# The expert layer's down product in plain f32 with stationary weights, with four weight and six activation buffers

## The chip, the core and the metric

The kernel runs on one NeuronCore of one Trainium2 chip. The metric is device time in microseconds of one launch, as the median of repeated runs. Engine names are those of the profile: PE is TensorE's matmul row and PEld its weight loads, DVE is VectorE, ACT is ScalarE, POOL is GpSimd, SP is the engine that issues most transfers.

## What is computed

Two transformer blocks on 256 tokens of width 2048, in f32: a hybrid mixer, then the expert layer (PEER), then a block with a pooling branch and a block with sparse attention. The change is in the expert layer. Cut to what matters:

```
hn = rms_norm(h) * gain                                  # 256 x 2048
idx, gates = top-k routing of hn @ w_query               # 8 heads x 16 experts of 16384
u = expert_down[idx]                                     # rows of 16384 x 2048
act = gelu(einsum('thkd,td->thk', u, hn))
out = einsum('thk,thkd->td', gates * act, expert_up[idx])
h = h + out
```

## The kernel before

Matmul operands are f32 values, split for speed: `split_w` (lines 149 to 165) loads a weight tile of 128 x 4 x 512 (1 MB) into a buffer `wr`, rounds it with ACT to a high part `wh` in the type float32r, and lets DVE subtract that from the original to get the low part `wl`, in two halves of 128 x 1024 each. Activations exist as a high and a low part too. `mm3` (line 167) then makes three matmuls, low x high, high x low, high x high, with the activations stationary (128 x 128) and 512 weight columns moving.

In the expert layer the first 192 tokens (TD) are computed densely over all 16384 experts, and the other 64 by gathering the rows of their chosen experts (`gathers`: indirect transfers on POOL's queue, a 128 x 2048 row tile each from the pool `fm`, 64 of the down rows, then 64 of the up rows, each consumed by one DVE instruction, lines 780 and 795). The dense part has 32 down chunks (`down`) of 512 experts, each four weight tiles long (2048 rows in four groups of 512), and 16 `up` blocks, each eight weight tiles long. Tokens 0 to 127 take `mm3`. Tokens 128 to 191 are only 64, so their high and low parts stand side by side in one stationary operand of 128 columns (`pack_hn` makes these, in three tiles of `fm`), and two matmuls do for four products (`product2`, lines 199 to 221): 20 matmuls of 512 columns per weight tile. The result has tokens on partitions. ACT copies it out with each token's normaliser (`inv`, and `inv_pair` for the paired layout), and `down_post` transposes it into expert-major form on PE, the pair folded by a matmul against `ff`, before ACT's Gelu writes it. The first seven pairs of chunks (LAG = 7) go out to DRAM (`S`, "hidden") on SP's queue and come back later; the others stay in the pool `gl`.

A gate table for the dense tokens is built by `gate_table` (DVE comparisons, PE products, 12 writes to DRAM) after the routing (`topk`, DVE for the most part). `prep` multiplies it into the activations and splits them for `up`.

Order: after the query product, 18 down chunks (72 tiles), during which routing, gate table and the first gathers run; then seven times an up block followed by two down chunks; then nine up blocks. Instructions are put in order by a planner which takes program order as priority, lets each engine run ahead where its inputs and buffers are ready in its own estimate of time, and issues weight transfers early (`high_priority`). On the chip each engine then keeps that order. A step between weight tiles (`step`, line 223) drives the routing, the gathers (PUMP) and the modulation weights of the second block (`mod_steps`), whose tiles share the `wr` buffers. Buffers before: `wr` 3, `wh` and `wl` 3 halves each, `fm` 7, `gl` 6, and four PSUM accumulators.

Of the kernel before, what the change touches and what calls it, by code (L numbers as in the profile page):

```python
# [10 lines left out]
F32 = mybir.dt.float32  # L11
# [4 lines left out]
AF = mybir.ActivationFunctionType  # L16
OP = mybir.AluOpType
# [4 lines left out]
T = 256  # L22
# [5 lines left out]
TD = 192  # L28
# [9 lines left out]
class Kern:  # L38
    def __init__(self, tc, ctx, d):
        self.tc, self.nc, self.d = tc, tc.nc, d  # L40
        pool = lambda name, bufs, **kw: ctx.enter_context(tc.tile_pool(name=name, bufs=bufs, **kw))
        self.cst = self.ph = pool("cst", 1)
        self.wr = pool("wr", 3)
        self.whp = pool("wh", 3)
        self.wlp = pool("wl", 3)
        self.fmp = pool("fm", 7)
        self.gl = pool("gl", 6)
        self.s4 = pool("s4", 4)
        self.s2 = pool("s2", 4)
        self.sm = pool("sm", 2)  # L50
        self.k1 = pool("k1", 4)
        self.mdp = pool("md", 1)
        self.accp = pool("acc", 4, space=PSUM)
        self.trp = pool("tr", 2, space=PSUM)
        self.msp = pool("ms", 2, space=PSUM)
        self.cnt = 0
        self.consts()
        self.mods = self.mod_steps()
        self.posts, self.seq, self.bg_rate, self.bg_due, self.nmods = [], [], 0.0, 0.0, 0
        self.pump, self.credit = None, 0.0  # L60
# [88 lines left out]
    def split_w(self, wsrc, i):  # L149
        nc = self.nc  # L150
        wr = self.wr.tile([128, 4, 512], F32, tag="wr", name=self.nm("wr"))
        hp = self.tc.high_priority(offset=self.prio)
        hp.__enter__()
        nc.sync.dma_start(wr.rearrange("p k n -> p (k n)"), wsrc[i])
        hs, ls = [], []
        for j in range(2):
            s = slice(2 * j, 2 * j + 2)
            wh = self.whp.tile([128, 2, 512], F32R, tag="wh", name=self.nm("wh"))
            nc.scalar.activation(wh, wr[:, s], AF.Copy)  # L159
            wl = self.wlp.tile([128, 2, 512], F32R, tag="wl", name=self.nm("wl"))  # L160
            nc.vector.tensor_tensor(wl, wr[:, s], wh.bitcast(F32), op=OP.subtract)  # L161
            hs += [wh[:, 0], wh[:, 1]]
            ls += [wl[:, 0], wl[:, 1]]
        hp.__exit__(None, None, None)
        return hs, ls

    def mm3(self, ps, xh, xl, wh, wl, first, last):
        mm = self.nc.tensor.matmul
# [635 lines left out]
    def peer(self, h):  # L804
# [5 lines left out]
        nc.vector.tensor_reduce(s1, self.ss_hn, axis=AX.X, op=OP.add)  # L810
        inv = self.c([128, 2], "inv2")
        self.rinv(inv, s1, 2, 1.0 / D)
        invp = self.c([128, 1], "inv_pair")
        nc.gpsimd.dma_start(invp[0:64], inv[0:64, 1:2])
        nc.gpsimd.dma_start(invp[64:128], inv[0:64, 1:2])
        R = self.c([128, 3, 2, 128], "route")
        ff = self.t_k1([128, 192])
        nc.gpsimd.memset(ff, 0.0)
# [4 lines left out]
        S = self.tc.dram_tile([LAG, 128, 8, TD], F32, name="hidden")  # L823
        C, act = {}, {}

        def down_post(c, tm):
            yield
            i, q = c // 2, c % 2
            if i < LAG:
# [1 line left out]
            else:  # L831
                if q == 0:
                    act[i] = self.t_gl([128, 8, TD])
                dst = act[i][:, 4 * q:4 * q + 4]
            for k in range(0, 4, 2):
                p = self.p_tr().rearrange("p (k t) -> p k t", k=2)
                for j in range(2):
                    ks = slice((k + j) * 128, (k + j + 1) * 128)
                    nc.tensor.transpose(p[:, j, 0:128], tm[0][:, ks], self.ident)
                    nc.tensor.matmul(p[:, j, 128:TD], tm[1][:, ks], ff[:, 64:128], start=True, stop=True)  # L840
                nc.scalar.activation(dst[:, k:k + 2], p[:, :, 0:TD], AF.Gelu)
            if i < LAG:
                nc.sync.dma_start(S[i, :, 4 * q:4 * q + 4], dst)

        def down(c):
            ps = [self.p_acc(), self.p_acc()]
            self.product2(ps, [(d["down"], c * 4 + g, hx[g * 4:g * 4 + 4]) for g in range(4)])
            tm = [self.t_s2([128, 512]) for _ in range(2)]
            nc.scalar.activation(tm[0], ps[0], AF.Copy, scale=inv[:, 0:1])
            nc.scalar.activation(tm[1], ps[1], AF.Copy, scale=invp)  # L850
            self.post(down_post(c, tm))

        def prep(p):
            if p < LAG:
# [54 lines left out]
            for k, p in self.tposes(lambda t, k: tm[t][:, k * 128:(k + 1) * 128], 0, 4):  # L909
                nc.scalar.activation(qf[c // 2][:, c % 2 * 4 + k], p, AF.Copy)  # L910

        hx = self.pack_hn(self.hn_tiles)
        for c in range(4):
            ps = self.linear(hn, d["peer_query"], c)
            tm = [self.t_s2([128, 512]) for _ in range(2)]
# [33 lines left out]
                down(2 * (LAG + 2 + i) + 1)  # L949
        self.finish()  # L950

    def pack_hn(self, hn):

        xh, xl, xp = (self.t_fm([128, 16, 128]) for _ in range(3))
        cp = lambda o, i: self.nc.scalar.activation(o, i.bitcast(F32), AF.Copy)
        for b, (h, l) in enumerate(hn):
            ks = slice(b * 8, b * 8 + 8)
            cp(xh[:, ks], h[:, :, 0:128])
            cp(xl[:, ks], l[:, :, 0:128])
            cp(xp[:, ks, 0:64], h[:, :, 128:TD])  # L960
            cp(xp[:, ks, 64:128], l[:, :, 128:TD])
        return [(xh[:, k], xl[:, k], xp[:, k]) for k in range(16)]

    def row_inv(self, x, name, n=D):
        nc = self.nc
# [332 lines left out]
    def dsa_attention(self, h, out, x, w, chunk_fm, neg):  # L1298
# [5 lines left out]
        for c in range(4):  # L1304
            chunk_fm(6 + c, 4, 16, kf[c // 2][:, c % 2 * 4:c % 2 * 4 + 4])
        v = [self.t_fm([128, D], F32) for _ in range(2)]
        of = [self.t_gl([128, 8, T]), self.t_fm([128, 8, T], F32)]
        scale = 128 ** -0.5
        pts = {}

# [33 lines left out]
        def values(c):  # L1344
            for hp in (2 * c, 2 * c + 1):
                yield
                p = self.p_ms().rearrange("p (j t) -> p j t", j=2)
                pt = pts.pop(hp)
                for j in range(2):
# [153 lines left out]
```

## Time and profile before

| | us |
|---|---|
| median of 3 runs | 2774.44 (2774.32 to 2775.48) |
| profiled execution, its time | 2777.65 |
| its span | 2775.9 |
| expert layer's weight tiles on PE, first to last | about 524 to 1884 |

The profile is of one execution. Busy time of an engine is the sum of its instructions' durations; a matmul's duration contains the pipeline's latency, so that consecutive matmuls overlap in it, and the distance between their starts says more. A plain f32 matmul shows as two records. Idle time in front of an instruction is put down to what it waited for last. The DMA share is the mean busy share of the core's 16 DMA engines; q0 is the queue of the gathers, q1 that of SP.

### The profile page before, as it was taken

How to read it: one execution, taken by the hardware profiler on the slowest of the kernel's cores; microseconds unless marked ns; L12 is line 12 of the kernel's file. 1: busy time of each engine (PE TensorE's matmuls, PEld its weight loads, DVE VectorE, ACT ScalarE, POOL GpSimd, SP SyncE). 2: the span in 40 equal slices, each digit the busy share in tenths (PEclk: the TensorE clock that was granted, in tenths of full speed). 3: DMA queues.
4: the chain of work that ended last, by engine and by line, in shares of the span. 5: the costliest groups of instructions: out<-in, count | busy, mean ns of one | idle time of the engine just before them, and what ended most of it. 6: DMA issues, size and time to landing. Idle time of an engine off the chain costs nothing.

```text
span 2775.9 us, 33244 instructions
## 1 busy us (share of the span) xinstructions
PE 2642.5 (95%) x12296; PEld 2142.0 (77%) x12296; DVE 2244.1 (81%) x3162; ACT 1394.2 (50%) x1881; POOL 271.3 (10%) x210
## 2 busy tenths in 40 slices
PE   8999999998998999999999899998999799999998
PEld 6787778877876777787877677777887687888886
DVE  6988886999997898768998789967779867765655
ACT  5547555554654444454544444444444444455543
POOL 1000000001112222102322212000000000000000
PEclk9999999999999999999999999999999899999999
DMA  7666675557999999869999999765788855655554
GB/s 291 261 224 227 259 261 203 195 202 265 382 374 398 358 372 373 320 238 334 406 366 374 353 363 357 291 224 219 277 304 324 310 201 193 226 208 187 182 194 170
DMA packets 135123, 782.08 MB, mean 282 GB/s; under 512 B 14000, under 2 KB 38736, under 8 KB 43760
## 3 DMA queue, kind: packets, MB, share of 16 engines
q1 hardware_dynamic: 113680, 639.81, 62.4%
q0 software_dynamic: 20752, 138.53, 12.8%
q8 instruction: 96, 1.57, 0.2%
q10 hardware_dynamic: 528, 1.61, 0.2%
q14 instruction: 67, 0.55, 0.1%
HBM read 759.11 MB, written 20.23 MB: 281 GB/s over the span
## 4 chain that ended last, share of the span: by engine, by line
PE 64%; DVE 14%; DMA 13%; issue 4%; ACT 3%; POOL 0%; ACTq 0%; DVEq 0%; POOLq 0%; SPq 0%
PE acc L170 16%; PE acc L171 16%; PE acc L169 16%; DVE wl L161 6%; PE acc L219 5%; PE acc L220 5%; DMA wr<-in_down 4%; DMA wr<-in_up 4%; ACT wh L159 2%; DMA wr<-in_mod_w 2%; DVE md L1014 1%; PE tr L267 1%; DVE gl L795 1%; DVE fm L780 1%; DMA wr<-in_pool_w_out 1%
## 5 line engine op out<-in xcount | busy, mean ns | idle before, releaser
L159 ACT ACTIVATE wh<-wr 128x1024 fp32r<-128x1024 f32 x944 | 991.4, 1058 | 1127.1 <-PE acc L171 380.7
L161 DVE TENSOR_TENSOR wl<-wr,wh 128x1024 fp32r<-128x1024 f32 x944 | 1140.5, 1220 | 408.2 <-ACT wh L159 398.9
L170 PE MATMUL acc<-wl,fm 128*128 128x512 f32 x1952 | 775.0, 397 | 29.5 <-DVE wl L161 28.7
L169 PE MATMUL acc<-wh,fm 128*128 128x512 f32 x1952 | 780.6, 402 | 16.4 <-ACT wh L159 14.4
L171 PE MATMUL acc<-wh,fm 128*128 128x512 f32 x1952 | 768.3, 394 | 0.0
L170 PEld LDWEIGHTS acc<-wl,fm 128*128 128x128 f32 x1952 | 370.5, 190 | 124.1 <-DVE wl L161 50.7
L169 PEld LDWEIGHTS acc<-wh,fm 128*128 128x128 f32 x1952 | 369.5, 190 | 95.5 <-ACT wh L159 18.8
L171 PEld LDWEIGHTS acc<-wh,fm 128*128 128x128 f32 x1952 | 370.1, 190 | 75.0
L170 PE MATMUL acc<-wl,gl 128*128 128x512 f32 x768 | 307.9, 401 | 18.6 <-DVE wl L161 18.6
L169 PE MATMUL acc<-wh,gl 128*128 128x512 f32 x768 | 305.2, 398 | 10.6 <-ACT wh L159 9.4
L171 PE MATMUL acc<-wh,gl 128*128 128x512 f32 x768 | 302.6, 394 | 0.0
L1014 DVE SCALAR_TENSOR_TENSOR md<-wr,c_c,md 128x1024 f32<-128x1024 f32 x180 | 230.4, 1280 | 35.4 <-DMA wr<-in_mod_w 33.4
L219 PE MATMUL acc<-wh,s 128*128 128x512 f32 x512 | 202.8, 396 | 0.0
L220 PE MATMUL acc<-wl,s 128*128 128x512 f32 x512 | 202.7, 396 | 0.0
L219 PE MATMUL acc<-wh,fm 128*128 128x512 f32 x512 | 202.2, 395 | 0.0
L220 PE MATMUL acc<-wl,fm 128*128 128x512 f32 x512 | 202.0, 395 | 0.0
L170 PEld LDWEIGHTS acc<-wl,gl 128*128 128x128 f32 x768 | 145.2, 189 | 63.9 <-DVE wl L161 31.8
L169 PEld LDWEIGHTS acc<-wh,gl 128*128 128x128 f32 x768 | 145.0, 189 | 46.0 <-ACT wh L159 12.2
L772 POOL DMA_INDIRECT fm<-in_up_rows,slot_rows x64 | 124.0, 1938 | 482.1 <-DVE gl L795 257.0
L171 PEld LDWEIGHTS acc<-wh,gl 128*128 128x128 f32 x768 | 145.5, 189 | 31.7 <-issue 1.0
L795 DVE SCALAR_TENSOR_TENSOR gl<-fm,slot_act,gl 128x2048 f32<-128x2048 f32 x63 | 147.7, 2344 | 6.1 <-DMA fm<-in_up_rows,slot_rows 6.1
L780 DVE SCALAR_TENSOR_TENSOR fm<-fm,gl 128x2048 f32<-128x2048 f32 x64 | 146.1, 2284 | 0.2 <-DMA fm<-in_down_rows,slot_rows 0.2
(416 smaller groups left out, 2377.6 us busy)
## 6 DMA issues: line engine op xcount, KB each, us to landing
wr<-in_down SPq DMA_DIRECT2D x128, 1024.0 KB, 8.6
wr<-in_up SPq DMA_DIRECT2D x128, 1024.0 KB, 8.1
wr<-in_mod_w SPq DMA_DIRECT2D x96, 1024.0 KB, 5.2
wr<-in_attn_w_in SPq DMA_DIRECT2D x72, 1024.0 KB, 4.8
wr<-in_w_in SPq DMA_DIRECT2D x44, 1024.0 KB, 5.2
wr<-in_pool_w_in SPq DMA_DIRECT2D x32, 1024.0 KB, 5.3
wr<-in_w_out SPq DMA_DIRECT2D x16, 1024.0 KB, 4.8
wr<-in_peer_query SPq DMA_DIRECT2D x16, 1024.0 KB, 4.7
```

Source lines behind the costliest of these rows:

```text
L159: nc.scalar.activation(wh, wr[:, s], AF.Copy)
L161: nc.vector.tensor_tensor(wl, wr[:, s], wh.bitcast(F32), op=OP.subtract)
L169: mm(ps, xl, wh, start=first, stop=False)
L170: mm(ps, xh, wl, start=False, stop=False)
L171: mm(ps, xh, wh, start=False, stop=last)
L219: mm(ps[1], xp, h, start=st, stop=False)
L220: mm(ps[1], xp, l, start=False, stop=sp)
L267: self.nc.tensor.transpose(p[:, j, t * 128:(t + 1) * 128], src(t, k + j), self.ident)
L772: nc.gpsimd.indirect_dma_start(rows[j], None, d[src], bass.IndirectOffsetOnAxis(ap=ei[:, j:j + 1], axis=0))
L780: nc.vector.scalar_tensor_tensor(r, r, 1.0, x2, op0=OP.mult, op1=OP.mult, accum_out=act[:, j - 2:j - 1])
L795: nc.vector.scalar_tensor_tensor(acc, r, c, acc, op0=OP.mult, op1=OP.add)
L1014: nc.vector.scalar_tensor_tensor(acc, w[:, j], cd[:, k:k + 1], acc, op0=OP.mult, op1=OP.add)
```

## The change

- Weight tiles of the down product are no longer split: `whole_w` loads the f32 tile, and `product_t` uses its 128 x 128 blocks as stationary operand, with the 192 tokens of the activations moving: for each of four rows-of-128 and four expert blocks one plain f32 matmul, 16 per tile. The result has experts on partitions, two blocks of 128 x 192 per accumulator.
- `whole_hn` makes the f32 activations from high and low part on DVE (two tiles of `fm` instead of three) and multiplies the normaliser in, which two small matmuls spread over the partitions. `pack_hn` and `inv_pair` with its two transfers go.
- `down_post` has no transposes; ACT's Gelu reads the accumulators. The copies out of PSUM go.
- `wr` has four buffers instead of three, `fm` six instead of seven.
- In the attention of the last block the second half of the output `of` comes from `gl` instead of `fm`, and is allocated when the fifth pair of heads begins.
- The up product, the gathers, the gate table and the order of the blocks are as before.

```diff
-        self.wr = pool("wr", 3)
+        self.wr = pool("wr", 4)
-        self.fmp = pool("fm", 7)
+        self.fmp = pool("fm", 6)
...
+    def whole_w(self, wsrc, i):
+        wr = self.wr.tile([128, 4, 512], F32, tag="wr", name=self.nm("wr"))
+        with self.tc.high_priority(offset=self.prio):
+            self.nc.sync.dma_start(wr.rearrange("p k n -> p (k n)"), wsrc[i])
+        return wr
+
+    def product_t(self, ps, groups):
+        n = len(groups)
+        for gi, (src, i, xs) in enumerate(groups):
+            w = self.whole_w(src, i)
+            for kk in range(4):
+                for e in range(4):
+                    self.nc.tensor.matmul(ps[e // 2][:, e % 2, :], w[:, kk, e * 128:(e + 1) * 128], xs[kk],
+                                          start=gi == kk == e % 2 == 0, stop=gi == n - 1 and kk == 3 and e % 2 == 1)
+            self.step()
...
-        invp = self.c([128, 1], "inv_pair")
-        nc.gpsimd.dma_start(invp[0:64], inv[0:64, 1:2])
-        nc.gpsimd.dma_start(invp[64:128], inv[0:64, 1:2])
...
-        def down_post(c, tm):
+        def down_post(c, ps):
...
-            for k in range(0, 4, 2):
-                p = self.p_tr().rearrange("p (k t) -> p k t", k=2)
-                for j in range(2):
-                    ks = slice((k + j) * 128, (k + j + 1) * 128)
-                    nc.tensor.transpose(p[:, j, 0:128], tm[0][:, ks], self.ident)
-                    nc.tensor.matmul(p[:, j, 128:TD], tm[1][:, ks], ff[:, 64:128], start=True, stop=True)
-                nc.scalar.activation(dst[:, k:k + 2], p[:, :, 0:TD], AF.Gelu)
+            for b in range(2):
+                nc.scalar.activation(dst[:, 2 * b:2 * b + 2], ps[b], AF.Gelu)
...
         def down(c):
-            ps = [self.p_acc(), self.p_acc()]
-            self.product2(ps, [(d["down"], c * 4 + g, hx[g * 4:g * 4 + 4]) for g in range(4)])
-            tm = [self.t_s2([128, 512]) for _ in range(2)]
-            nc.scalar.activation(tm[0], ps[0], AF.Copy, scale=inv[:, 0:1])
-            nc.scalar.activation(tm[1], ps[1], AF.Copy, scale=invp)
-            self.post(down_post(c, tm))
+            ps = [self.p_acc()[:, 0:2 * TD].rearrange("p (e t) -> p e t", e=2) for _ in range(2)]
+            self.product_t(ps, [(d["down"], c * 4 + g, hx[g * 4:g * 4 + 4]) for g in range(4)])
+            self.post(down_post(c, ps))
...
-        hx = self.pack_hn(self.hn_tiles)
+        hx = self.whole_hn(self.hn_tiles, inv)
...
+    def whole_hn(self, hn, inv):
+        nc = self.nc
+        p = self.p_ms()[:, :T]
+        for t in range(2):
+            nc.tensor.matmul(p[:, t * 128:(t + 1) * 128], inv[:, t:t + 1].to_broadcast([128, 128]), self.ident,
+                             start=True, stop=True)
+        row = self.t_k1([128, TD])
+        nc.scalar.activation(row, p[:, :TD], AF.Copy)
+        out = []
+        for h, l in hn:
+            x = self.t_fm([128, 8, TD], F32)
+            nc.vector.tensor_tensor(x, h[:, :, 0:TD].bitcast(F32), l[:, :, 0:TD].bitcast(F32), op=OP.add)
+            nc.vector.tensor_tensor(x, x, row[:, None, :].to_broadcast([128, 8, TD]), op=OP.mult)
+            out += [x[:, k] for k in range(8)]
+        return out
...
-        of = [self.t_gl([128, 8, T]), self.t_fm([128, 8, T], F32)]
+        of = [self.t_gl([128, 8, T])]
...
+                if hp == 4:
+                    of.append(self.t_gl([128, 8, T]))
```

## Rows read from the trace of the kernel before

**Rows 1.** The page: busy time of the engines, and DMA in 40 slices.

```profile
PE 2642.5 (95%) x12296; PEld 2142.0 (77%) x12296; DVE 2244.1 (81%) x3162; ACT 1394.2 (50%) x1881; POOL 271.3 (10%) x210
...
DMA  7666675557999999869999999765788855655554
```

**Rows 2.** The page: the chain that ended last, by engine.

```profile
PE 64%; DVE 14%; DMA 13%; issue 4%; ACT 3%; POOL 0%; ACTq 0%; DVEq 0%; POOLq 0%; SPq 0%
```

**Rows 3.** Stretches, line 220 alone: us, PE (count), PEld (count), clock, DMA, GB/s.

```profile
524.00:655.00 131.00, 37.72 (x96) 18.16 (x96) 0.97 0.60 208
655.00:825.00 170.00, 42.88 (x107) 20.54 (x107) 0.96 0.94 360
825.00:951.00 126.00, 33.66 (x85) 16.25 (x85) 0.97 0.97 383
951.00:1518.00 567.00, 176.26 (x448) 84.63 (x448) 0.99 0.91 347
1518.00:1884.00 366.00, 114.15 (x288) 54.68 (x288) 0.98 0.84 318
```

**Rows 4.** Timeline of PE: start us, us, instruction; 20 matmuls apart.

```profile
639.65 0.39 PE L169 MATMUL acc<-wh,fm 128*128 128x512 f32 x1
...
644.18 0.39 PE L169 MATMUL acc<-wh,fm 128*128 128x512 f32 x1
```

**Rows 5.** Timeline of PE: a chunk's transposes, then a burst of the gate table.

```profile
671.78 0.27 PE L839 MATMUL tr<-ident,s 128*128 128x128 f32 x1
...
672.91 1.09 PE L732 MATMUL ms<-s,s 128*128 128x128 f16 x16
673.81 0.47 PE L169 MATMUL acc<-wh,fm 128*128 128x512 f32 x1
```

**Rows 6.** Timeline of PE, two stretches with plain f32 matmuls.

```profile
470.52 1.95 PE L639 MATMUL ms<-gl,gl 128*128 128x128 f32 x16
...
472.54 0.40 PE L170 MATMUL acc<-wl,fm 128*128 128x512 f32 x1
...
1838.97 1.88 PE L800 MATMUL ms<-gl,k 128*128 128x512 f32 x4
...
1840.91 0.40 PE L170 MATMUL acc<-wl,gl 128*128 128x512 f32 x1
```

**Rows 7.** Groups by line, shapes apart: busy us, mean ns; idle before, releasers.

```profile
L161 DVE TENSOR_TENSOR wl<-wr,wh 128x1024 fp32r<-128x1024 f32 x944 | 1140.5, 1220 | 408.2 <-ACT wh L159 398.9 <-PE acc L219 4.9 <-PE acc L220 1.4
L159 ACT ACTIVATE wh<-wr 128x1024 fp32r<-128x1024 f32 x944 | 991.4, 1058 | 1127.1 <-PE acc L171 380.7 <-PE acc L219 287.6 <-DMA wr<-in_up 113.4
...
L780 DVE SCALAR_TENSOR_TENSOR fm<-fm,gl 128x2048 f32<-128x2048 f32 x64 | 146.1, 2284 | 0.2 <-DMA fm<-in_down_rows,slot_rows 0.2
...
L639 PEld LDWEIGHTS ms<-gl,gl 128*128 128x128 f32 x64 | 7.8, 191 | 0.3
```

**Rows 8.** Waits from 700 to 1130: us in total, times, longest.

```profile
POOL fm L772 <- DVE fm L780: 303.8, 53, 13.2
...
PEld acc L170 <- DVE wl L161: 37.6, 31, 7.4
```

**Rows 9.** Waits from 524 to 655.

```profile
PE tr L839 <- ACT s L849: 4.5, 1, 4.5
```

**Rows 10.** The chain of waits in order of time, from 820: start us, us, what.

```profile
839.66 12.93 DMA wr<-in_down
```

**Rows 11.** DMA from 825 to 925: queue q0 (packets, MB, share), then issues.

```profile
q0 software_dynamic: 2295, 16.75, 42.7%
...
wr<-in_down SPq DMA_DIRECT2D x17, 1024.0 KB, 11.3
...
fm<-in_down_rows,slot_rows POOLq DMA_INDIRECT x17, 10.5
```

**Rows 12.** DMA from 700 to 800: issues of the gathers.

```profile
fm<-in_down_rows,slot_rows POOLq DMA_INDIRECT x10, 11.3
```

**Rows 13.** Waits of SP, the queue of the weight transfers, whole span.

```profile
SPq L843 <- ACT s L841: 39.8, 11, 7.9
```

More of the change, by code (lines that the diff above doesn't have):

```diff
@@ L950, in peer @@
         self.finish()
[L952 to L962, printed above, removed]
+    def whole_hn(self, hn, inv):
[13 more added lines that the diff above has]
+        return out
     def row_inv(self, x, name, n=D):
```

## Prediction

> **What bounds the kernel now.** The page first [rows 1]: TensorE (PE) is busy 95% and VectorE (DVE) 81%, and the DMA digits reach 9 over the slices of the expert layer, about 650 to 1750 us. The chain of work that ended last runs for 64% of the span through PE, but for 14% through DVE and 13% through DMA [rows 2]. So PE is the bound, with waits in it, and the question for this change is what those waits are and whether PE gets more work.
>
> Busy time on PE contains pipeline latency, so I counted tiles instead. One 1 MB weight tile is 20 matmuls, and where nothing is late 20 of them take 644.18 - 639.65 = 4.53 us [rows 4]. Line 220 runs four times a tile, so its counts divided by 4 are tiles [rows 3]. The expert layer has three parts: 524 to 951 with 72 down tiles, 951 to 1518 with 56 down and 56 up tiles, 1518 to 1884 with 72 up tiles. Other PE work in them: a down chunk's transposes, 672.91 - 671.78 = 1.13 us, 18 and 14 times; 24 bursts of the gate table, 673.81 - 672.91 = 0.90 us each [rows 5]; in the third part the folding products, 16 records of 0.43 us (below), 7 us.
> - First part: 72 x 4.53 + 20 + 22 = 368 of 427 us, 59 lost.
> - Second: 112 x 4.53 + 16 = 523 of 567, 44 lost.
> - Third: 72 x 4.53 + 7 = 333 of 366, 33 lost.
>
> That is 136 us of waiting in the layer. Its causes: in the first 131 us PE waits once for 4.5 us for ScalarE's (ACT) copy before the transposes [rows 9]; later PE's loads wait for the low half from DVE, 37.6 us in 31 pieces [rows 8], and the chain shows why: a weight buffer comes free when DVE has read it, the transfer then takes 12.93 us [rows 10], and both splits follow. DMA is busy 0.94 to 0.97 from 655 to 951 [rows 3].
>
> **The change, part by part.**
>
> *PE, down tiles.* Removed: 20 matmuls, 4.53 us. Added: 16 plain f32 matmuls of 192 columns. Their price is not in the trace at that width, but both neighbours are. A plain f32 matmul leaves two records. Sixteen records of 128 columns run from 470.52 to 0.23 us before the record at 472.54, so 1.79 us, 0.112 each (0.23 is the spacing of the split matmuls, 4.53/20); four of 512 columns from 1838.97 to 0.23 before 1840.91, so 1.71 us, 0.428 each [rows 6]. Every record has a weight load of its own, 64 for the 32 matmuls of line 639 [rows 7], and they hide. By columns alone 192 cost 0.428 x 192/512 = 0.160; on the line between the neighbours 0.112 + (64/384) x 0.316 = 0.165. A tile is 32 records: 5.13 to 5.27 us, and I take 5.2, between two close ends. So PE gets 0.67 us more per down tile, 128 x 0.67 = +86 us, and loses the transposes, 32 x 1.13 = -36: +50 us of PE work. This part of the change is a loss; the gain has to come out of the 136 us.
>
> *DVE and ACT.* A down tile no longer costs two subtractions of 1.22 us on DVE and two copies of 1.06 us on ACT [rows 7]: 312 and 271 us less. Neither engine is the bound, so this is worth only what it takes out of PE's waits: a down matmul now waits for its transfer alone. The ACT copies of the sums go too; the Gelus stay, reading PSUM directly, and hold two of the four accumulators a little longer, hidden under the next chunk's 20 us.
>
> *Buffers.* A weight buffer was free once DVE had read it; now, for a down tile, when PE has done 16 matmuls. With a fourth buffer, four tiles per transfer (12.93 us in [rows 10]) plus 5.2 us of use is 18.1/4 = 4.5 us a tile, under 5.2. So the ring keeps up with PE if transfers do not get slower than about 15 us. Activations shrink from three buffers to two while the pool loses one, so the gathers still have four.
>
> *SP's queue.* The write of the hidden activations still waits there for the Gelu, 39.8 us in 11 pieces [rows 13], and weight transfers are queued behind it. The transposes ahead of the Gelu are gone, so this gets shorter; with a spare buffer I cost it at 0, and at up to 7.9 us, its longest, if one lands badly.
>
> *New set-up.* Four DVE operations of 1536 elements replace eight copies on ACT: 4 x 1.22 x 1536/1024 = 7.3 us at the rate of the subtraction [rows 7], beside the query product. Two small matmuls wait on PE for the normaliser, and the query's matmuls are queued behind them: 0 to 5 us by the nearest wait, 4.5 us [rows 9]. I take 2 for both, as the first down tile comes a whole product later. The two tiny pair transfers that go are off every path.
>
> *Other stages.* A fourth weight buffer also serves all split products; PE's waits there are not in these rows. Between -12 (a tenth of what waits cost in the expert layer) and +5 (the later allocation of the attention output, or an unlucky new order, by the same 4.5 us wait); I take -6.
>
> *Sum.* PE floors: first part 72 x 5.2 + 22 = 396; second 56 x (4.53 + 5.2) = 545; third 333; together 1274 against 1224. Waits that stay, of 136:
> - First part 20 of 59. 524 to 655 loses 15 (131 less 24 tiles and six chunks' transposes), from ACT and DVE while DMA is at 0.60, and keeps 2. 655 to 951, with DMA at 0.94 to 0.97, keeps 18 of 44: PE asks for weights more slowly, the transfers do not get faster.
> - Second 12 of 44: the up tiles' waits for their splits stay.
> - Third 18 of 33: up tiles alone, helped by the buffer only.
>
> 1274 + 50 = 1324 against 1360: -36. With +2 and -6, -40. The profiled execution took 2777.65 us, 3.2 above the median, so 2737.6 there and 2734.4 at the median.
>
> **The rivals.**
>
> 1. *The waits go almost wholly.* If the lost time was DVE's lateness and not DMA, some 15 of 136 us stay: 1274 + 15 = 1289, -71, with -4 elsewhere 2699. For it: 37.6 us of waits for DVE [rows 8]. Against: DMA at 0.97 [rows 3].
>
> 2. *The waits only change their name.* Where DMA is full a fourth buffer buys nothing, as gathers and weights share it. From 825 to 925, 17 weight tiles and 17 gathers were issued and the gathers' queue held 42.7% of the DMA time [rows 11]: 5.9 us a tile, more than 5.2. If waits fall only by the 50 us that PE now works, the result is 2774. [...]
>
> 3. *Gathers run ahead: slower.* DVE, freed of splits, frees the gathers' buffers sooner (GpSimd waits 303.8 us for the 2.28 us multiply that releases them [rows 7, 8]), so they run at 17 per 100 us already while the gate table is written, where it was 10 [rows 12]. Over the 170 us from 655 that is 12 gathers early, 12 weight tiles late: 12 x 5.2 = 62 us on the first part. What comes back when those gathers are missing later is 12 x 1.05 MB at 383 GB/s [rows 3], 33 us of DMA time, of which perhaps half is in a full stretch. -40 + 62 - 16 = +6, and +20 if nothing comes back: 2780 to 2795. It decides from about 8 gathers early (40/5.2).
>
> 4. *The f32 stream is slower than its neighbours show*, for instance bound by the 0.19 us of a weight load [rows 7]: 32 x 0.19 = 6.1 us a tile, 128 x 0.9 = +115, about 2850. Against it: 0.112 us records with a load each [rows 6].
>
> **How the numbers follow.** Forecast 0.48, rival 1 0.15, rival 2 0.17, rival 3 0.17, rival 4 0.03. About 0.2% (5.5 us) is what a measurement of this kernel can tell from no change, so faster means under 2769 and slower over 2780. Faster: nearly all of 0.48, 0.15, and a third of rival 2: 0.67. Same: half of rival 2 and a little of the forecast: 0.10. Slower: rivals 3 and 4 and the rest of rival 2: 0.23. The range runs from 2695, which cuts off the better half of rival 1, to 2797, the end of rival 3.
>
> **What would show it.** Right: plain f32 records starting 0.160 to 0.165 us apart in the first part, so 5.1 to 5.3 us a tile; no PE wait for ACT before 655; the first part at 410 to 425 us, the second at 550 to 565, the third at 340 to 355. Rival 1: the first part under 405. Rival 2: the first part at 427 with PE waiting for the transfers of down tiles. Rival 3: many more gathers issued by the end of the first part than before, and that part over 445 us. The prediction is wrong if the tile takes over 5.5 us, if the order on DVE makes up tiles later, or if stages outside the layer move by over 12 us.

## The result, and the profile after

| | us | ratio to the kernel before, 95% interval |
|---|---|---|
| before, median of 4 | 2774.38 (2769.45 to 2775.48) | |
| after, median of 4 | 2859.59 (2848.54 to 2863.60) | 1.0302 [1.0281, 1.0323] |
| after, profiled execution | 2848.54, span 2846.8 | |

The kernel became 3% slower; the forecast was 2735, and the time lies above the range's upper end of 2797. Its page, engines and the DMA digits (compare [rows 1]):

```profile
PE 2677.7 (94%) x13452; PEld 2305.9 (81%) x13452; DVE 1961.2 (69%) x2910; ACT 1094.9 (38%) x1556; POOL 228.3 (8%) x208
...
DMA  8666775569989886669987899765778965665554
```

DVE's busy time fell by 283 us (2244.1 to 1961.2), near the forecast's 312 less 7. PE's rose by 35 us, but the time rose by 85, so something waits besides. The profiled execution is the fastest of the four, 11 us under their median. The stretches tell where (us, busy time of each engine with its count of instructions, granted clock, DMA share, GB/s). Down tiles alone run to 985, the alternating part to 1602, the last up tiles to 1957:

```profile
524.00:655.00 131.00, 131.00 (x823) 130.96 (x822) 82.25 (x361) 16.18 (x29) 6.03 (x7) 1.00 0.65 232
655.00:850.00 195.00, 162.37 (x1181) 159.06 (x1181) 131.15 (x167) 31.97 (x62) 35.65 (x29) 0.92 0.94 377
850.00:985.00 135.00, 121.91 (x726) 120.16 (x726) 52.60 (x50) 10.89 (x20) 19.70 (x19) 0.96 0.93 354
985.00:1317.00 332.00, 318.67 (x1666) 288.83 (x1665) 156.06 (x155) 80.23 (x95) 25.96 (x19) 0.98 0.74 278
1317.00:1602.00 285.00, 251.03 (x1251) 222.68 (x1250) 178.17 (x147) 64.44 (x79) 55.35 (x36) 0.93 0.88 335
1602.00:1957.00 355.00, 342.40 (x1454) 272.55 (x1452) 295.74 (x294) 167.96 (x184) 42.33 (x25) 0.99 0.84 312
```

Until 655 PE is never idle. The first multiplies of gathered rows run at about that time, and from 655 to 985 and from 1317 to 1602 PE stands and works at a lower granted clock (0.92, 0.96 and 0.93). The three parts took about 463, 617 and 355 us, where they took 427, 567 and 366 before [rows 3].

Groups by line in the page (busy us, mean ns, idle time before them and what ended it) show what is new on DVE: waits in front of the two multiplies of gathered rows.

```profile
L798 DVE SCALAR_TENSOR_TENSOR fm<-fm,gl 128x2048 f32<-128x2048 f32 x64 | 146.2, 2290 | 169.4 <-DMA fm<-in_down_rows,slot_rows 169.4
...
L813 DVE SCALAR_TENSOR_TENSOR gl<-fm,slot_act,gl 128x2048 f32<-128x2048 f32 x63 | 148.0, 2348 | 85.9 <-DMA fm<-in_up_rows,slot_rows 85.7
```

In the kernel before, the first of them waited 0.2 us for its rows [rows 7] and the second 6.1 us (waits from 520 to 1960: us in total, times, longest):

```profile
DVE gl L795 <- DMA fm<-in_up_rows,slot_rows: 6.1, 6, 1.8
```

Now DVE stands, idle in front of an instruction, 169.4 us for down rows and 85.7 us for up rows. PE's waits over the same stretch say who is queued behind:

```profile
PE acc L188 <- DVE wl L161: 53.4, 20, 8.3
PE ms L750 <- DVE s L764: 32.6, 9, 10.2
PE acc L181 <- DMA wr<-in_down: 11.3, 4, 8.0
```

A down tile hardly waits for its transfer (11.3 us). The gate table's products (L750) wait for DVE's comparisons (L764), the up products for DVE's subtractions (L161). The timeline of all engines shows one such wait (start us, us, instruction, idle time before it):

```profile
705.08 2.29 DVE L798 SCALAR_TENSOR_TENSOR fm<-fm,gl 128x2048 f32<-128x2048 f32 x1 [2.58 <-DMA fm<-in_down_rows,slot_rows]
...
709.34 2.29 DVE L798 SCALAR_TENSOR_TENSOR fm<-fm,gl 128x2048 f32<-128x2048 f32 x1 [0.76 <-DMA fm<-in_down_rows,slot_rows]
...
713.46 2.29 DVE L798 SCALAR_TENSOR_TENSOR fm<-fm,gl 128x2048 f32<-128x2048 f32 x1 [1.81 <-DMA fm<-in_down_rows,slot_rows]
...
715.68 1.29 DVE L764 TENSOR_TENSOR s<-s,slot_major 128x1024 f16<-128x1024 f16 x2
...
716.42 0.29 PE L750 MATMUL ms<-s,s 128*128 128x128 f16 x1 [10.17 <-DVE s L764]
```

and in the alternating part the same with a subtraction:

```profile
1402.21 2.35 DVE L813 SCALAR_TENSOR_TENSOR gl<-fm,slot_act,gl 128x2048 f32<-128x2048 f32 x1 [6.48 <-DMA fm<-in_up_rows,slot_rows]
...
1407.00 2.35 DVE L813 SCALAR_TENSOR_TENSOR gl<-fm,slot_act,gl 128x2048 f32<-128x2048 f32 x1 [2.44 <-DMA fm<-in_up_rows,slot_rows]
1409.26 2.35 DVE L161 TENSOR_TENSOR wl<-wr,wh 128x1024 fp32r<-128x1024 f32 x2
1410.54 0.80 PE L188 MATMUL acc<-wl,gl 128*128 128x512 f32 x1 [5.75 <-DVE wl L161]
1411.13 0.63 PE L189 MATMUL acc<-wh,gl 128*128 128x512 f32 x1
...
1411.56 0.63 PE L237 MATMUL acc<-wh,s 128*128 128x512 f32 x1
...
1416.25 0.41 PE L238 MATMUL acc<-wl,s 128*128 128x512 f32 x1
1416.50 0.39 PE L187 MATMUL acc<-wh,gl 128*128 128x512 f32 x1
```

DVE stands for a row, with work for PE behind it in its queue. But standing is only a part of the lateness: of PE's 10.17 us in the first example DVE stood for 2.6 and multiplied for about 5.5. The comparison started right behind the third multiply (713.46 + 2.29, then 715.68), with no idle time of its own in front. Over the layer PE waits 87 us for DVE, and in that time DVE stands for rows for 22 us, multiplies for 29 and does other, overdue work for 34. After its wait in the second example PE works on at a granted clock of 0.50 (1410 to 1416): matmuls of 512 columns start 0.43 us apart (1411.13 to 1411.56) and from 1416.25 on 0.25 us.

The size fits roughly: 32.6 us of waits for comparisons and 8% of 195 us, 16 us, for the granted clock of 0.92 in 655 to 850, then 11 us for transfers and 4% of 135 us, 5 us, for the 0.96 in 850 to 985, make 65 us for a first part that is 58 us longer than without gathers (405, below). In the alternating part PE is idle for 13 us up to 1317 and 34 us from there; with 7% of 285, 20 us, for the 0.93 there, that is 67 us for 68. The lower clock is counted here as if it were granted only while PE works; it was 0.50 from 710 to 716.4 too, with PE idle, so these sums run a little high. The 20 us that the last part is longer than without gathers were not traced.

That gave theory A: *multiplies stand in DVE's queue ahead of work that PE needs, and wait there for rows that are late*. Its rivals: B, the gathers' share of the DMA slows the weights (rival 3 of the prediction); C, ACT's order or the buffers, with no part of the gathers.

### The profile page after: what moved, and what is told of

It is laid out like the page before. It is cut to its first block, busy times and chain, and to the rows that moved or that the text cites. A ratio compares the mean times of both kernels' runs of the same rounds, so it can differ in the third digit from the quotient of the medians.

```text
span 2846.8 us, 34504 instructions
## 1 busy us (share of the span) xinstructions
PE 2677.7 (94%) x13452; PEld 2305.9 (81%) x13452; DVE 1961.2 (69%) x2910; ACT 1094.9 (38%) x1556; POOL 228.3 (8%) x208
## 5 line engine op out<-in xcount | busy, mean ns | idle before, releaser
L161 DVE TENSOR_TENSOR wl<-wr,wh 128x1024 fp32r<-128x1024 f32 x688 | 835.7, 1221 | 352.9 <-ACT wh L159 349.7
L159 ACT ACTIVATE wh<-wr 128x1024 fp32r<-128x1024 f32 x688 | 725.2, 1059 | 861.1 <-PE acc L189 455.3
L181 PE MATMUL acc<-fm,wr 128*128 128x192 f32 x4096 | 682.2, 329 | 11.9 <-DMA wr<-in_down 11.3
L181 PEld LDWEIGHTS acc<-fm,wr 128*128 128x128 f32 x4096 | 673.6, 192 | 14.2 <-DMA wr<-in_down 12.5
L187 PE MATMUL acc<-wh,fm 128*128 128x512 f32 x1440 | 574.9, 400 | 9.8 <-ACT wh L159 9.8
L188 PE MATMUL acc<-wl,fm 128*128 128x512 f32 x1440 | 567.1, 394 | 2.5 <-DVE wl L161 2.4
L189 PE MATMUL acc<-wh,fm 128*128 128x512 f32 x1440 | 565.9, 393 | 0.0
L187 PEld LDWEIGHTS acc<-wh,fm 128*128 128x128 f32 x1440 | 271.7, 189 | 65.9 <-ACT wh L159 10.9
L188 PEld LDWEIGHTS acc<-wl,fm 128*128 128x128 f32 x1440 | 272.5, 189 | 61.6 <-DVE wl L161 6.8
L189 PEld LDWEIGHTS acc<-wh,fm 128*128 128x128 f32 x1440 | 272.1, 189 | 56.4
L798 DVE SCALAR_TENSOR_TENSOR fm<-fm,gl 128x2048 f32<-128x2048 f32 x64 | 146.2, 2290 | 169.4 <-DMA fm<-in_down_rows,slot_rows 169.4
L813 DVE SCALAR_TENSOR_TENSOR gl<-fm,slot_act,gl 128x2048 f32<-128x2048 f32 x63 | 148.0, 2348 | 85.9 <-DMA fm<-in_up_rows,slot_rows 85.7
L790 POOL DMA_INDIRECT fm<-in_up_rows,slot_rows x64 | 107.6, 1682 | 575.0 <-DVE gl L813 245.3
```

What stands on the lines that cost most here:

```text
L181: self.nc.tensor.matmul(ps[e // 2][:, e % 2, :], w[:, kk, e * 128:(e + 1) * 128], xs[kk], start=gi == kk == e % 2 == 0, stop=gi == n - 1 a ...
L187: mm(ps, xl, wh, start=first, stop=False)
L188: mm(ps, xh, wl, start=False, stop=False)
L189: mm(ps, xh, wh, start=False, stop=last)
L790: nc.gpsimd.indirect_dma_start(rows[j], None, d[src], bass.IndirectOffsetOnAxis(ap=ei[:, j:j + 1], axis=0))
L798: nc.vector.scalar_tensor_tensor(r, r, 1.0, x2, op0=OP.mult, op1=OP.mult, accum_out=act[:, j - 2:j - 1])
```

## Experiments

Medians in us; where an interval is given, the ratio is to runs of the kernel before on the same chip.

**1. Both kernels without gathers.**

```diff
-            self.pump = self.gathers(h, R, inv, x2, ff)
-            next(self.pump)
+            self.pump = None
...
-                for _ in self.pump:
-                    pass
+                pass
```

> The changed kernel without its 128 row gathers: their transfers, their multiplies on DVE and the four small products at their end are left out, so the last 64 tokens get no expert output. Theory A (DVE keeps its order, so gate comparisons and the up tiles' subtractions stand behind multiplies that wait for gathered rows) and theory B (the gathers take DMA bandwidth from the weights) both expect PE's waits in the expert layer to go almost wholly: the layer at 1295 to 1310 us instead of 1435, the total near 2715. Theory C (the gathers have nothing to do with it; the new ACT order, Gelus that wait for PE, or the buffers hold up the splits) expects a layer over 1380 and a total over 2790.

> The kernel before without the same work, as the control. Theories A and B: the layer at 1250 to 1280 us instead of 1360 and the total near 2690, as 50 us less of PE work than in the changed kernel stand against some 25 us of waits for ACT and DVE. If the total is above that of the changed kernel without gathers, the change is a gain as such and only the gathers spoil it; if it is below, it is a loss as such by the difference.

Measured, one execution each: after 2703.61, before 2678.87. So the gathers, with all that hangs on them, cost the kernel after 156 us and the kernel before 95, and C falls. Stretches of the kernel after without gathers, its three parts (columns as above):

```profile
523.00:928.00 405.00, 405.00 (x2744) 403.08 (x2743) 150.91 (x484) 60.33 (x113) 0.82 (x2) 1.00 0.70 244
928.00:1477.00 549.00, 549.00 (x2913) 501.38 (x2912) 215.68 (x237) 147.16 (x175) 0.00 (x0) 1.00 0.67 236
1477.00:1812.00 335.00, 335.00 (x1446) 270.63 (x1444) 244.01 (x260) 164.68 (x181) 1.57 (x3) 1.00 0.74 258
```

and of the kernel before without gathers:

```profile
523.00:919.00 396.00, 385.71 (x2082) 320.93 (x2081) 316.89 (x624) 225.20 (x289) 0.24 (x1) 0.98 0.71 251
919.00:1447.00 528.00, 528.00 (x2402) 435.18 (x2401) 343.03 (x340) 276.25 (x308) 0.00 (x0) 1.00 0.69 243
1447.00:1784.00 337.00, 336.18 (x1459) 271.98 (x1457) 251.31 (x273) 170.22 (x192) 2.16 (x4) 1.00 0.73 261
```

After, PE is busy without a gap at a granted clock of 1.00: 1289 us is its floor. Before, the layer takes 1261 us, only 37 over the prediction's floor of 1224. So some 99 of the 136 us of waits came with the gathers and not with the splits, and without gathers the change just costs work on PE: 24.7 us.

**2. Multiplies held to their place in the program.** Each goes behind every DVE instruction that stands earlier in the program, and no longer where the planner thinks its row has come. (The first multiply of the up rows, another instruction, stays free.)

```diff
-                nc.vector.scalar_tensor_tensor(r, r, 1.0, x2, op0=OP.mult, op1=OP.mult,
-                                               accum_out=act[:, j - 2:j - 1])
+                self.tc.keep_in_program_order(nc.vector.scalar_tensor_tensor(
+                    r, r, 1.0, x2, op0=OP.mult, op1=OP.mult, accum_out=act[:, j - 2:j - 1]))
...
-                    nc.vector.scalar_tensor_tensor(acc, r, c, acc, op0=OP.mult, op1=OP.add)
+                    self.tc.keep_in_program_order(nc.vector.scalar_tensor_tensor(
+                        acc, r, c, acc, op0=OP.mult, op1=OP.add))
```

> The changed kernel with each multiply of a gathered row held behind every DVE instruction that comes before it in program order; nothing else changes. The multiplies can then not be planned ahead of gate comparisons and subtractions that the program has first. Theory A: DVE's waits for gathered rows fall from 255 us to under 120, PE's waits for the gate comparisons and the low halves fall by half or more, total 2760 to 2800. Theory B: transfers compete as before, total 2835 to 2870.

> The kernel before, with the same two multiplies of gathered rows held to their place in the program on VectorE (nothing left out). Theory A (the change lets VectorE stand behind multiplies that wait for gathered rows; the kernel before hardly has such waits, 6.3 us in all): 2758 to 2777 us, a gain of 0 to 16. If the pin were a general gain, unconnected with the change, it would bring the kernel before as much as the kernel after, 97 us: 2670 to 2700. If the pin has a cost of its own (rows wait in their buffers, gathers come later): over 2780.

> The kernel after with only the multiply of the down rows pinned, that of the up rows free. If each set of gathers does its own harm in its own part: the first part as in the fully pinned kernel, 430 to 440 us, the alternating part as in the kernel after, 605 to 625 us, so 2815 to 2840 us. If the harm of the alternating part is only the late end of the down gathers handed on: alternating part 550 to 570, total 2760 to 2790.

Measured: after pinned 2762.48, ratio 0.9967 [0.9949, 0.9985]; before pinned 2747.91, 0.9887 [0.9865, 0.9910]; after with the down multiply alone pinned 2818.98, 1.0147 [1.0128, 1.0167]. Stretches of the pinned kernel after, its three parts:

```profile
524.00:958.00 434.00, 410.83 (x2740) 406.90 (x2739) 212.25 (x535) 59.45 (x112) 36.89 (x33) 0.98 0.79 298
958.00:1510.00 552.00, 549.95 (x2914) 501.61 (x2913) 346.04 (x331) 146.04 (x173) 104.76 (x63) 1.00 0.91 349
1510.00:1867.00 357.00, 344.04 (x1452) 274.53 (x1450) 332.44 (x309) 167.31 (x185) 60.28 (x38) 0.99 0.93 356
```

The alternating part is back at its floor, 552 us against 549, with more gathers in it (63 instructions of POOL against 55) and more DMA (0.91 against 0.81): there the order on DVE did the harm, and not the load on the DMA. In the first part the pin also moves gathers to later (33 instructions of POOL against 55), so that more than one thing changes. 97 us of the 156 come back. With the up multiply free the first part takes 436 us and the alternating part still 614, so each set of gathers does its harm in its own part. That the kernel before gained 30 us too was not expected (at most 16). Its PE waits for the low half, before and then with the pin:

```profile
PE acc L170 <- DVE wl L161: 44.2, 50, 7.0
```

```profile
PE acc L170 <- DVE wl L161: 17.3, 25, 2.3
```

DVE hardly stood for rows there (6.3 us), so that the place of the multiplies, 2.28 us each, ahead of subtractions is the likely cause; no run shows it alone. With the pin in both, the change costs 0.9967 against 0.9887, some 22 us: about what it costs without gathers.

**3. The buffers of before**, in the kernel after and in the pinned one.

```diff
-        self.wr = pool("wr", 4)
+        self.wr = pool("wr", 3)
-        self.fmp = pool("fm", 6)
+        self.fmp = pool("fm", 7)
```

> The changed kernel with the buffers as before: three for weights, seven for activations, so that the gathers have five rows in flight instead of four. If the fourth weight buffer or the sixth activation buffer is what costs, the total falls under 2800. Theory A: no gain, 2840 to 2880, since one more gather in flight brings more multiplies forward; theory B: the same or slower, 2850 to 2890, as weights lose a transfer in flight to the gathers.

> The pinned kernel after with three weight buffers and seven activation buffers, as before the change. If the fourth weight buffer earns what the prediction gave it (some 30 us of waits for transfers): 2785 to 2800. If it is worth what it was without the pin, 16 us: 2773 to 2783. If the down tiles' short use of a buffer makes it needless: 2755 to 2768.

Measured: 2875.3, 1.0362 [1.0331, 1.0393], and pinned 2795.52, 1.0065 [1.0044, 1.0086]. By the ratios the fourth weight buffer, bought with the seventh activation buffer, is worth 17 us unpinned and 27 pinned. The buffers are not the cause.

**4. Gathers alone, multiplies alone.** The pin might also work by holding back gathers, which need the buffers that the multiplies free. So each half was run by itself, unpinned: gathers whose rows nobody reads, and multiplies of a tile that is there already.

```diff
+        for src in ("down_rows", "up_rows"):
+            for j in range(66):
+                if j < 64:
+                    issue(src, j)
+                yield
```

```diff
-                issue("down_rows", j)
+                rows[j] = self.t_fm([128, D], F32)
...
-                nc.vector.scalar_tensor_tensor(r, r, 1.0, x2, op0=OP.mult, op1=OP.mult,
+                nc.vector.scalar_tensor_tensor(r, x2, 1.0, x2, op0=OP.mult, op1=OP.mult,
...
-                issue("up_rows", j)
+                pass
...
-                r = rows.pop(j - 2)
+                r = x2
```

The first diff's loop stands in place of both loops of `gathers`.

> The kernel after with its 128 gathers as they are, and the multiplies of the gathered rows left out, with the small products behind them (tokens 192 to 255 get no expert output); nothing pinned. No instruction of VectorE waits for a gathered row here, the transfers are all there. Theory A (VectorE's order): 2735 to 2765 us, that is at most what the gathers still cost in the pinned kernel, 59 us over the 2704 without them. Theory B (the gathers' share of the DMA): 2835 to 2870, as the kernel after.

> The kernel after with its 128 multiplies on VectorE (2.29 us each, 293 us in all) free to be placed anywhere, but of a row that is there already; the gathers are left out (tokens 192 to 255 get a wrong expert sum). Theory A in its narrow form (the wait for the row does the harm, not the place of the multiply): 2704 to 2735 us. If the 2.29 us that a multiply placed too early takes from comparisons and subtractions do it: 2790 to 2860.

Measured: gathers alone 2850.38, multiplies alone 2724.68. The second is as A has it: placed freely, 128 multiplies cost 21 us if their data are there. (The planner orders each of these kernels anew, so a multiply does not stand in the same place in all of them.) The first spoke against A: no instruction on DVE waits for a row, and the harm is as large. But the waits of SP (SyncE) in that kernel (520 to 1960) show a new stand: the gate table's reads (L846 there) need a buffer that gathers hold, and the weight transfers are queued behind them, 158 us.

```profile
SPq L846 <- DMA fm<-in_up_rows,slot_rows: 131.3, 14, 25.6
...
SPq L846 <- DMA fm<-in_down_rows,slot_rows: 26.6, 2, 25.0
```

**5. Pace and queues, to tell these apart.** Three causes were open: A, DVE's order; B', gathers that run ahead of their planned pace and crowd the DMA; C', SP's stand. Paced: ahead of each gather a copy of its index column onto itself, held to its place on DVE. The gather reads that column, so it can't start before the copy.

```diff
+            at = ei[:, j:j + 1]
+            self.tc.keep_in_program_order(nc.vector.tensor_copy(at, at))
             nc.gpsimd.indirect_dma_start(rows[j], None, d[src],
                                          bass.IndirectOffsetOnAxis(ap=ei[:, j:j + 1], axis=0))
```

Queues moved: the reads to GpSimd's queue, the writes of hidden activations to ScalarE's.

```diff
-            nc.sync.dma_start(g8, G[:, :, 8 * p:8 * p + 8, :].rearrange("g p i t -> p g i t"))
+            nc.gpsimd.dma_start(g8, G[:, :, 8 * p:8 * p + 8, :].rearrange("g p i t -> p g i t"))
...
-                nc.sync.dma_start(S[i, :, 4 * q:4 * q + 4], dst)
+                nc.scalar.dma_start(S[i, :, 4 * q:4 * q + 4], dst)
```

> The kernel after, its multiplies free as they were; a copy of each gather's index column onto itself, held to its place in the program on VectorE, goes ahead of the gather, so that no gather starts before its turn. B' (gathers that run ahead crowd out the weights): first part 425 to 440 us, 10 to 14 gathers from 655 to 755 us where the kernel after has 22, total 2750 to 2785. A (VectorE stands at multiplies whose rows are late): VectorE still stands over 100 us for rows, 2800 to 2860. Both, B' in the first part and A in the alternating one: first part 425 to 440, alternating part still 600 to 620, total 2805 to 2835.

> The kernel with its gathers alone (multiplies of the rows left out, tokens 192 to 255 get no expert output), the gathers paced by the same copies. B': 2730 to 2765 us, where the unpaced one took 2850. If 128 gathers of 1 MB cost what they cost however they are paced: 2835 to 2860.

> The kernel with its gathers alone, unpaced (multiplies of the rows left out, tokens 192 to 255 get no expert output), and the gate table's reads on GpSimd's queue, the writes of the hidden activations on ScalarE's. SyncE stood 158 us there for buffers that gathers held. C' (that stand is the harm): 2720 to 2790. B': the first part stays at 440 to 455 us, total 2800 to 2850, with the gathers' share of the DMA unchanged.

> The kernel after with the same two queues moved, nothing pinned or paced. C': below 2800 us. A or B': 2840 to 2862, at most the 8 us that this move brought the pinned kernel and a few more.

| kernel after with | multiplies left out | multiplies free |
|---|---|---|
| nothing else | 2850.38 | 2859.59 |
| gathers paced | 2771.66 | 2861.01, 1.0316 [1.0273, 1.0360] |
| queues moved | 2758.20 | 2880.53, 1.0378 [1.0322, 1.0435] |

The left column: most of the harm of gathers without multiplies comes through SP's queue or their early start; either cure takes 79 or 92 us away, and 68 or 55 stay. The right column: neither cure brings the kernel itself down. In the paced one DVE still stands for rows (waits of 520 to 1960):

```profile
DVE fm L800 <- DMA fm<-in_down_rows,slot_rows: 214.6, 54, 11.1
DVE gl L815 <- DMA fm<-in_up_rows,slot_rows: 103.9, 33, 10.7
```

With the queues moved the kernel takes longer than every theory had it. Its largest new wait is on PE, for ACT's rounding of an up tile:

```profile
PE acc L187 <- ACT wh L159: 49.5, 3, 42.6
```

In those 42.6 us (974 to 1017) DVE stands at multiplies of down rows (over the layer 205.7 us in 53 waits, the longest 32.2). Behind them in its queue is the gate multiplication of an `up` block (L872), for which ACT's rounding of the activations waits, and behind that in ACT's queue the rounding of the weights. That is A once more, by way of ACT.

Part by part, from the first matmul of a part's tiles on PE to the last (us, one execution each):

| kernel after with | down tiles alone | alternating | last up tiles |
|---|---|---|---|
| neither gathers nor multiplies | 403 | 549 | 336 |
| multiplies alone | 416 | 551 | 339 |
| gathers alone, queues moved | 421 | 551 | 367 |
| gathers alone, paced | 429 | 551 | 371 |
| both | 460 | 619 | 354 |
| both, queues moved | 450 | 667 | 354 |
| both, paced | 443 | 603 | 394 |
| both, multiplies pinned | 433 | 552 | 358 |

In the alternating part neither half costs more than 2 us and both together cost 70. In the first part it is mixed: 13 us of the 57 come with the multiplies alone and 18 with the gathers alone, and pacing wins back 17. In the paced kernel the last part, 40 us longer, eats up what the other two gain; so its total speaks against B', its first part in some measure for it.

B' in the first part is read from the DMA from 655 to 755, the gathers' queue (packets, MB, share) and the issues of weight tiles and gathers (count, KB, median us to landing). First the kernel after, then gathers alone with the queues moved:

```profile
q0 software_dynamic: 3167, 23.01, 56.6%
...
wr<-in_down SPq DMA_DIRECT2D x11, 1024.0 KB, 13.9
...
fm<-in_down_rows,slot_rows POOLq DMA_INDIRECT x22, 15.1
```

```profile
q0 software_dynamic: 2852, 20.78, 50.0%
...
fm<-in_down_rows,slot_rows POOLq DMA_INDIRECT x20, 20.3
```

Nearly the same number of gathers, twice the 10 of [rows 12], holds half the DMA in both. Yet the first part takes only 421 us in the second kernel, against 460 in the kernel after. So of the harm there some 18 us can be B' and 13 the multiplies' own time, and the rest needs both. In total: neither 2703.61, multiplies alone 2724.68 (+21), gathers alone with the queues moved 2758.20 (+55), both 2880.53 with the queues moved (+177), 2859.59 as it stands (+156). A holds: multiplies that wait for gathers, in front of work that PE needs. How much of it is the standing and how much the multiply's place, the runs don't separate.

C' is real, but not what sets the time of the kernel after. There SP stands 79 us for the buffers of the gate table's reads, and with the multiplies pinned still 75, at 97 us less. First the kernel after, then the pinned one (520 to 1960):

```profile
SPq L867 <- DVE fm L798: 36.9, 3, 20.8
...
SPq L867 <- DVE gl L813: 23.7, 10, 4.5
SPq L867 <- DMA fm<-in_up_rows,slot_rows: 18.5, 4, 8.9
```

```profile
SPq L868 <- DVE gl L813: 40.3, 11, 5.1
SPq L868 <- DVE fm L798: 34.8, 4, 22.2
```

**6. A better version?** What the pinned kernels still lose:

> The pinned kernel after, and the gate table's reads are issued from GpSimd's queue, the writes of the hidden activations from ScalarE's, both SyncE's before. In the pinned kernel SyncE stands 34.8 us in 4 waits for a buffer that a multiply of gathered rows frees, with weight transfers behind it, and TensorE then stands 12.1 us at 863 us and works on at half clock. Theory A in its wider form (whatever waits in order for gathered rows holds up the weights): that stall and its slow stretch go, first part 412 to 425 us instead of 433, total 2738 to 2755. If DMA bandwidth sets the first part: no change, 2758 to 2768.

> The kernel before with the two multiplies pinned, and the writes of the hidden activations and of the gate table issued from ScalarE's queue, right behind the operations that make their data, instead of SyncE's. In the pinned kernel before SyncE stands 32.1 us and 26.5 us for these (11 waits each, longest 7.1 us) with weight transfers queued behind. If a wait of SyncE there reaches TensorE: 2735 to 2745 us. If the three weight buffers cover it: 2745 to 2751, no difference from the pinned kernel before.

> As the pinned kernel before with the two writes on ScalarE's queue, and the gate table's reads on GpSimd's queue too, the same moves that made the pinned kernel after 8 us faster. If SyncE's waits matter alike in both kernels: 2735 to 2745. If they matter in the kernel after alone, where a down tile asks for a weight buffer as soon as TensorE lets it go: 2745 to 2755, and the reads, which stand behind gathers on GpSimd, come later: VectorE then waits for them, some 28 us in all as in the pinned kernel after with queues moved.

Measured: the pinned kernel after with queues moved 2754.20, 0.9913 [0.9896, 0.9930], 8 us less by the medians and 15 by the ratios. Its first part is about 415 us instead of 433, as SP no longer stands; in the pinned kernel the timeline showed how PE waits for the weights issued behind the read:

```profile
863.05 0.38 SPq L868 DMA_DIRECT2D fm<-gates  x1
863.53 1.82 SPq L170 DMA_DIRECT2D wr<-in_down  x3
...
875.83 4.53 PE L181 MATMUL acc<-fm,wr 128*128 128x192 f32 x13 [12.13 <-DMA wr<-in_down]
```

In the kernel before nothing is gained: with the writes alone moved 2744.54, 0.9889 [0.9868, 0.9910], by the ratio no difference from its pinned form; with the reads moved too 2757.76, 0.9943 [0.9920, 0.9966], slower than the pinned form and than either expectation. So the best kernel found is the one before the change with its two multiplies pinned, 0.989 of its time; the change is not part of it.

## Why the prediction was wrong

- *The price of the f32 stream* was right. PE's timeline after shows 32 records between two bursts of the gate table:

```profile
673.58 5.42 PE L181 MATMUL acc<-fm,wr 128*128 128x192 f32 x32
678.83 1.10 PE L750 MATMUL ms<-s,s 128*128 128x128 f16 x16
```

  678.83 - 673.58 = 5.25 us a tile, 0.164 a record; 5.2 was taken. Rival 4 is out. "No PE wait for ACT before 655" held too: PE is busy for the whole stretch.
- *PE's floors* were 396, 545 and 333; without gathers they measured 405, 549 and 335, 15 us more in all. Of these the tile's 0.05 us makes 6; the other 9 were not traced.
- *The waits that stay* are the step that failed: 50 of 136 was forecast, and they became 1435 - 1289 = 146 (by the measured floor). I took PE's waits for the low half for lateness of the splits, and expected them to go with the splits. By experiment 1 most belonged to the gathers, and with those gone the change has little left to win. With the multiplies pinned 1343 - 1289 = 54 stay (29, 3 and 22 by parts, where 20, 12 and 18 were forecast): what was missing from the sum is the order on DVE.
- *DVE's release* was "worth only what it takes out of PE's waits". With the queue's order as it is, it was worth less than nothing. In the full queue of before, rows had landed by the time DVE came to their multiply (0.2 us of waiting, [rows 7]); with 283 us less in it, DVE came early and stood. From the issue of a gather to the start of its multiply it took a median of 18 us (down rows) and 27 us (up rows) before, 13 and 12 after, and 31 and 41 in the pinned kernel after; a gather landed after a median of 10.9 and 10.7 us before, 11.1 and 10.1 after. The prediction named "if the order on DVE makes up tiles later" as what would make it wrong, and gave it no price.
- *Rival 3* had the trigger (gathers running ahead, a first part over 445 us) and the sign, but the wrong mechanism: it charged the early gathers as DMA time, 62 us for the first part. By experiment 5 that is at most some 18 us there, and most of the harm lies with DVE.
- *Rival 2*, weights late behind gathers, shows as 11.3 us of PE's waits for down tiles. *Rival 1* is seen only where the gathers are gone.
- *Buffers*: right in kind; the exchange of buffers brought 17 to 27 us. *SP's queue*: at most 7.9 us was allowed for, and the writes were looked at; what stood there for 12 us (experiment 6) was the read beside them, which needs a buffer that the gathers hold.
- *Set-up and other stages*, +2 and -6: outside the layer's three parts the span fell from 2775.9 - 1360 = 1416 to 2846.8 - 1435 = 1412, so -4, the forecast's sum, but by luck: the first down tile started 3.2 us earlier (524.9 and 521.7) where +2 was forecast, and what lies behind the layer lost 1.3 where it was -6.

What stays open: why the planner's order fits the kernel before better, and where the last part's 20 us come from. The runs show the effect of the order, not how its estimates of a gather's landing come about.

## What to carry to other kernels

Work taken off an engine that is not the bound need not be a gain (here 283 us less on DVE went with 85 us more in all): look at what stands in its queue behind an instruction that waits for a transfer, because that wait was perhaps hidden by the very work that goes. Before crediting a change with waits, run the kernel without the suspected cause; here the kernel before without gathers would have shown that 99 of the 136 us came with the gathers. And where a planner orders an engine's queue, hold instructions that wait for slow transfers to their place in the program: it brought 30 us in the kernel before without any other change.

## What the runs showed of the hardware

- A plain f32 matmul of 192 columns cost 2 x 0.164 us on PE in the kernel after (5.25 us for 32 records), each record with a weight load of its own that hid: without gathers PE ran 549 us without a gap, with 2912 weight loads to 2913 matmul records.
- In the kernel after, PE worked on at a granted clock of 0.50 after its waits of 10.17 us (716.4 to 719.5) and of 5.75 us (1410.5 to 1416): matmuls of 512 columns started 0.43 us apart, then 0.25 us. From 1411.13 to 1416.25 that was 12 of them in 5.12 us, where 0.25 us apart makes 3.0, so the second wait cost some 2.1 us more than its length. The granted clock averaged 0.92 from 655 to 850 and 0.93 from 1317 to 1602, and 1.00 in all three parts without gathers.
- With many gathers in flight a weight tile's transfer took a median of 13.9 us to land and a gather 15.1 (655 to 755, 22 gathers issued, rows in experiment 5), while in the kernel with paced gathers, 8 of them in that time, they took 7.9 and 10.1:

```profile
wr<-in_down SPq DMA_DIRECT2D x15, 1024.0 KB, 7.9
...
fm<-in_down_rows,slot_rows POOLq DMA_INDIRECT x8, 10.1
```
